# Two layers of attention and product-key experts: activation and weight stores issued from ScalarE's queue, and a reordered attention of layer 1

## The chip, the cores and the metric

The kernel runs on one core of a Trainium2 chip. A core has TensorE (PE, matrix products), VectorE (DVE), ScalarE (ACT), GpSimd (POOL) and SyncE (SP), each with an instruction stream of its own that it runs in order, and 16 DMA engines that move data between HBM and the core's memory. Transfers are issued by an engine's stream: in this kernel SP's, ACT's and, for the indexed gathers, POOL's. The metric is the device time of one launch in microseconds, the median of several.

## What is computed

Two layers, each with an attention half and an expert half. The input is a latent stream of 512 tokens and a context of 256, both 1024 wide, all in 32-bit floats.

```python
for l in range(DEPTH):                    # DEPTH = 2
    last = l == DEPTH - 1
    ...                                   # sh1 .. g2, csh1 .. cg2: (silu(c) @ w_mod[l] + b_mod[l]), six parts
    hc = modulate(h_ctx, csh1, cs1)       # rms(x) * (1 + scale) + shift
    ...                                   # keys and values of the context; last: nothing else of it
    hx = modulate(x, sh1, s1)
    q, k, v, u = split_cols(hx @ w_in[l])
    q = apply_rope(rms(q...) * q_gain[l], cos, sin)
    k = apply_rope(rms(k...) * k_gain[l], cos, sin)
    o_attn = attend_latent(q, [kc, k], [vc, v])
    o_conv = conformer_conv(u, conv_w[l], conv_b[l], ln_g[l], ln_b[l])   # 31 taps
    x = x + g1 * merge_groups(o_attn, o_conv, beta_attn[l], beta_conv[l], w_o[l])
    x = x + g2 * peer(modulate(x, sh2, s2), peer_wq[l], peer_keys[l], peer_u[l], peer_v[l])
    if not last:
        ...                               # the same for the context
return rms(x) * final_g
```

`peer` picks, for each token and each of 8 heads, 16 of 16384 experts by the sum of two key scores. For each chosen expert e it adds `gelu(h . u[e]) * w[e] * v[e]`.

## The kernel before

`attention_layer(l, ...)` and `peer_layer(l, ...)` are called in turn for the two layers. Both write their work as generators ("streams") whose `yield` carries an estimated length; `merge` (L212) always advances the stream whose clock is lowest, each multiplied by a pace (`T0`, `T1`, `FD` and so on, L43 on). That fixes the order in which instructions are written; a scheduler of the compiler may still move them, after which each engine's order is fixed.

**The expert half** computes most tokens densely: products of all 16384 `u` rows with the tokens (the u stage), then weighted sums of all `v` rows (the v stage). Every 32-bit operand is split in a high and a low part and three products are summed. In layer 0 four tiles of 128 latent tokens go this way, in layer 1 three. The rest, the two context tiles in layer 0 and the last latent tile in layer 1, is gathered: for each of the 128 expert slots of a tile, POOL gathers rows `uv` (L896), DVE forms the dot product (L900), ACT the gelu (L901, L902) and DVE adds (L889).

The u stage (`u_stream`, L978 on) takes 128 chunks of 128 experts per layer. For a chunk SP loads `raw` (L986, 512 KB, two buffers), ACT casts it to `hi` (L989), POOL makes `lo` (L990), PE runs 24 products into `ups` (L994), ACT makes `ge` (L996, two buffers), and the result is stored to `gd` in HBM (L998, 256 KB in layer 0, 192 KB in layer 1, for 120 of the 128 chunks; the last eight stay on the core). The v stage reads `gd` and `wd` back.

Beside the u stage `w_stream` spreads the router's weights over the experts. For four tokens at a time DVE makes one-hot tables `o` (L955), ACT scales one of them (L960), PE multiplies both (`wps`, L961) and ACT copies the result into `sg` (L963). After 32 tokens the block of 2 MB is stored to `wd` (L965), 16 times in layer 0 (984.6 to 1480 us) and 12 times in layer 1 (3039 to 3460 us). All `raw` loads and all `gd` and `wd` stores are issued from SP's queue.

**The attention half.** At its start `rope`, `convw` and `gains` are loaded behind the three `wqkv` blocks (L278 to L286); from gains and rope DVE makes `gq` and the four tables `rot` (L289 to L296). Then `project` (L590) runs the projections, `taps` the convolution on DVE and partly GpSimd, `largest` the row maxima. In layer 1 `context_kv` (L575) computes keys and values of one context tile: a norm (`hC`), a row broadcast through `dg` and PE (`rows`, L196 and L197), and `qkv`. It is called for the first tile inside `project` and for the second after the merge, in one piece with high priority. `more_mods` computes the modulation vectors `mods[l, s]` (L127): products of `silu(c)` with streamed blocks `wm`. At the end `conv_norm` normalizes the convolution's output into `yhi` and `ylo`, `attend` writes the attention's output into `qs` as a high part (ACT, L485) and a low part (DVE, L486), and the loop at L692 multiplies both with the split output weights (`whi` on ACT, L618; `wlo` on POOL, L619).

Of the kernel before, what the change touches and what calls it, by code (L numbers as in the profile page):

```python
# [9 lines left out]
F32 = mybir.dt.float32  # L10
# [7 lines left out]
P = 128  # L18
D = 1024
KD = D // P  # L20
# [3 lines left out]
NL = SEQ // P  # L24
NT = T // P
HD = 64
# [12 lines left out]
EPS = 1e-6  # L39
# [5 lines left out]
T0 = (1.0, 1.0)  # L45
T1 = (2.0, 2.0)
CY = 2.0
# [13 lines left out]
def body(ctx: ExitStack, tc: tile.TileContext, io):  # L61
# [165 lines left out]
    def attention_layer(l, st, fgs, fp, mark):  # L227
# [18 lines left out]
        work = pool("awk", 2, hst)  # L246
        hT = hp.tile([P, KD, nq * P], F32, tag="hT", name="hT")
        TW = SEQ if last else GW - 2 * PAD
        parts = [] if last else [(1, CT, [hT[:, k, SEQ:] for k in range(KD)])]
# [30 lines left out]
        convw = mid.tile([P, 4, CONVK], F32, name="convw")  # L280
        gains = hp.tile([P, 2, HD], F32, name="gains")

        wqkv = [wload(io["w_qkv"][l, c], "wqkv") for c in range(3)]
        nc.sync.dma_start(convw, io["convw"][:, l])
        nc.sync.dma_start(rope, io["rope"].rearrange("(n p) c d -> p n c d", p=P))
        nc.sync.dma_start(gains, io["gains"][l].partition_broadcast(P))  # L286

# [201 lines left out]
        def more_mods():  # L489
            for m in (((0, 2), (0, 3), (0, 4), (0, 5), (1, 0), (1, 1)) if l == 0 else ((1, 2), (1, 3), (1, 4), (1, 5))):  # L490
                yield from mod(*m, ppt)

        def conv_norm(t0, n, g0):
# [29 lines left out]
            for b in range(4):  # L523
                if t0:
                    V.scalar_tensor_tensor(yT[:, b, ys], yT[:, b, ys], vecs[:, l, b, 4:5], bc, op0=ALU.mult, op1=ALU.mult)
                else:
# [7 lines left out]
                    V.tensor_tensor(out=lo[:, 0:SEQ].rearrange("p (j t) -> p j t", j=hi.shape[1]), in0=q, in1=hi.bitcast(F32), op=ALU.subtract)  # L534
                    ylo.append(lo[:, 0:SEQ])
            done.append("latent" if t0 == 0 else "context")
            yield 2.0
# [39 lines left out]
        def context_kv(i):  # L577

            x = xT[:, :, i * P:(i + 1) * P]
            A.activation(hC, x, AF.Square)  # L580
            bc = rows(rsqrt(col_sums([hC[:, k, :] for k in range(KD)], 1), 1, 1.0 / D, EPS, "n"), 1)
            V.tensor_tensor(out=hC, in0=x, in1=bc.unsqueeze(1).to_broadcast([P, KD, P]), op=ALU.mult)
            V.tensor_tensor(out=hC, in0=hC, in1=mods[l, 1][:, :, 1:2].to_broadcast([P, KD, P]), op=ALU.mult)
            V.tensor_tensor(out=hC, in0=hC, in1=mods[l, 0][:, :, 1:2].to_broadcast([P, KD, P]), op=ALU.add)
            for _ in qkv(i):
                pass

        def project():
            for i in LAT if last else CT + LAT:
                yield from qkv(i)  # L590
                if last and i == LAT[-1]:
                    context_kv(NL)
            if last:
# [11 lines left out]
        if last:  # L605
            clock["mod"] = 100.0
            del streams["conv"]
            merge({**streams, "fg": (fgs, FD), "mod": (md, 2.4)}, clock, ("p", "fg"))
            with tc.high_priority():
                context_kv(NL + 1)  # L610
        else:
            merge(streams, clock, ("p",))
# [80 lines left out]
        for hf in range(4):  # L693
            if hf == len(ws):
                ws.append(wo_split(hf, op.tile([P, KD, WC], F32R, tag="whi", name="whi"), op.tile([P, KD, WC], F32R, tag="wlo", name="wlo")))
            while len(opened) < len(ws):
                opened.append(pbig.tile([P, 2, SEQ], F32, tag="big", name="wo"))
                products(opened[-1], ws[len(opened) - 1], (4, 5, 6, 7))
            ps = opened[hf]
            products(ps, ws[hf], (0, 1, 2, 3))  # L700
# [6 lines left out]
    def peer_layer(l, fp):  # L707
# [6 lines left out]
        with ExitStack() as outer:  # L714
# [216 lines left out]
            def w_stream():  # L931

                for i in dd:
# [16 lines left out]
                    for blk in range(4):  # L950
                        sg = rw.tile([P, PK // 2, 32, 2], F32, tag="sg", name="sg", bufs=2)
                        for t0 in range(0, 32, 4):
# [11 lines left out]
                            yield 1.9  # L964
                        nc.sync.dma_start(wd[:, :, (i - dd[0]) * 4 + blk].rearrange("g p h t e -> p g (h t e)"), sg.rearrange("p (g h) t e -> p g (h t e)", h=2))  # L965

# [15 lines left out]
            def u_stream():  # L982

                for c in range(PK):
# [12 lines left out]
                    if c < PK - 8:  # L997
                        nc.sync.dma_start(gd[c // 4, :, c % 4], ge[:, 0:td])  # L998
                    else:
# [189 lines left out]
```

## Time and profile before

| what | us |
|---|---|
| median of 3 runs | 4179.64 (4172.8 to 4183.14) |
| the profiled execution | 4177.53 |
| its span | 4175.8 |
| layer 0: attention, u stage, v stage | 0 to 508, to 1572, to 2316 |
| layer 1: attention, u stage, v stage | 2316 to 2725, to 3555, to 4176 |
| busy: PE, DVE, POOL, ACT | 3769, 3098, 2217, 1812 |

The profile comes from one execution on the chip, whose own time stands in the second row. A row of the timeline names the start, the length, the engine, the line of the kernel, the operation, what it writes and reads, and in brackets how long the engine stood idle before it and what released it. An engine's name with a q (SPq, ACTq) means its instruction queue, where issues of transfers are seen. A row of the waits names who waited for what, how long in all, how often, and the longest. [...]

### The profile page before, as it was taken

The page shows a single profiled execution, that of the slowest core. Times are in us where ns is not written, and L with a number is a line of the kernel's source. Part 1 is how long each engine was busy: PE and PEld are TensorE (multiplying, and loading weights), DVE is VectorE, ACT ScalarE, POOL GpSimd, SP SyncE. Part 2 cuts the span into 40 slices and gives each one's busy share as a digit, 9 for nine tenths or more (in the row PEclk, how much of TensorE's full clock was granted, in tenths as well). Part 3 has the DMA queues.
Part 4 walks back from the last instruction along what each step waited for, and adds up shares of the span by engine and source line. Part 5 has one row for each costly group of instructions (what it writes and reads, how often), then busy time and mean ns, then how long its engine had stood idle before and what let it go on. Part 6 is the DMA issues. An engine that isn't in the chain of part 4 may idle for free. (4 is left out here: it accounts for less than half of the span.)

```text
span 4175.8 us, 54192 instructions
## 1 busy us (share of the span) xinstructions
PE 3769.0 (90%) x19278; PEld 3204.7 (77%) x19278; DVE 3098.4 (74%) x5680; ACT 1811.6 (43%) x3679; POOL 2216.7 (53%) x1223
## 2 busy tenths in 40 slices
PE   8879998989988999999999779889888989898998
PEld 6547776867777777888777547679888888898897
DVE  5693369999986647898887784389877453787885
ACT  3345233336675633333333246333466564333333
POOL 0580135666665456555556356135756555665664
PEclk9989999999999999999999889899999999999999
DMA  4142135987888888988887714046676878898884
GB/s 169 58 182 81 51 119 204 331 304 244 285 285 287 268 319 338 344 322 335 339 335 292 275 41 172 21 136 241 231 247 220 259 262 283 320 345 297 315 319 140
DMA packets 327631, 1003.72 MB, mean 240 GB/s; under 512 B 24384, under 2 KB 159808, under 8 KB 264256
## 3 DMA queue, kind: packets, MB, share of 16 engines
q1 hardware_dynamic: 266128, 580.25, 40.5%
q0 software_dynamic: 59904, 419.46, 27.1%
q8 instruction: 152, 2.49, 0.2%
q14 instruction: 119, 0.97, 0.1%
q10 hardware_dynamic: 1328, 0.55, 0.0%
HBM read 884.29 MB, written 115.87 MB: 240 GB/s over the span
## 5 line engine op out<-in xcount | busy, mean ns | idle before, releaser
L990 POOL TENSOR_TENSOR lo<-raw,hi 128x1024 fp32r<-128x1024 f32 x256 | 647.1, 2529 | 572.0 <-ACT hi L989 504.7
L1028 POOL TENSOR_TENSOR vlo<-vr,vhi 128x1024 fp32r<-128x1024 f32 x256 | 629.5, 2466 | 471.4 <-ACT vhi L1027 457.4
L1035 PE MATMUL vps<-ahi,vhi 128*128 128x512 f32 (+1 forms) x2048 | 759.7, 372 | 44.5 <-DVE xT L1038 26.5
L1035 PE MATMUL vps<-alo,vhi 128*128 128x512 f32 (+1 forms) x2048 | 757.4, 370 | 3.1 <-DVE alo L974 3.1
L1035 PE MATMUL vps<-ahi,vlo 128*128 128x512 f32 (+1 forms) x2048 | 740.2, 371 | 9.2 <-POOL vlo L1028 9.1
L900 DVE SCALAR_TENSOR_TENSOR uv<-uv,hp 128x1024 f32<-128x1024 f32 x363 | 439.7, 1211 | 212.2 <-DMA uv<-in_uv,uix 212.1
L994 PE MATMUL ups<-hhi,hi 128*128 128x512 f32 (+1 forms) x2048 | 504.9, 386 | 72.2 <-ACT ge L996 34.7
L889 DVE SCALAR_TENSOR_TENSOR yp<-uv,act,yp 128x1024 f32<-128x1024 f32 x359 | 460.4, 1283 | 144.9 <-ACT act L902 144.0
L896 POOL DMA_INDIRECT uv<-in_uv,uix x384 | 447.8, 1166 | 222.0 <-DVE y L889 45.4
L994 PEld LDWEIGHTS ups<-hhi,hi 128*128 128x128 f32 x2048 | 383.7, 198 | 127.6 <-ACT ge L996 41.3
L994 PE MATMUL ups<-hhi,lo 128*128 128x512 f32 (+1 forms) x2048 | 479.0, 371 | 1.8 <-POOL lo L990 1.8
L994 PE MATMUL ups<-hlo,hi 128*128 128x512 f32 (+1 forms) x2048 | 475.1, 370 | 0.0
L1035 PEld LDWEIGHTS vps<-ahi,vhi 128*128 128x128 f32 x2048 | 391.3, 191 | 99.8 <-DVE xT L1038 30.6
L1035 PEld LDWEIGHTS vps<-ahi,vlo 128*128 128x128 f32 x2048 | 389.7, 191 | 63.2 <-POOL vlo L1028 16.2
L1035 PEld LDWEIGHTS vps<-alo,vhi 128*128 128x128 f32 x2048 | 391.6, 191 | 51.4 <-DVE alo L974 4.4
L901 ACT ACTIVATE act<-dots 128x1 f32<-128x1 f32 x384 | 77.4, 202 | 803.5 <-DVE uv L900 802.5
L994 PEld LDWEIGHTS ups<-hlo,hi 128*128 128x128 f32 x2048 | 378.8, 192 | 40.5
L994 PEld LDWEIGHTS ups<-hhi,lo 128*128 128x128 f32 x2048 | 373.4, 191 | 40.6 <-POOL lo L990 2.4
L955 DVE TENSOR_TENSOR o<-iota,xf 128x1024 f32<-128x1024 f32 x224 | 385.9, 1749 | 21.0 <-ACT o L960 9.3
L410 POOL TENSOR_TENSOR yT<-yT,tp 128x512 f32<-128x512 f32 (+1 forms) x150 | 261.4, 1743 | 211.9 <-ACT tp L409 201.7
L989 ACT CAST hi<-raw 128x1024 fp32r<-128x1024 f32 x256 | 267.0, 1043 | 217.8 <-DMA raw<-in_uT 185.3
L960 ACT ACTIVATE o<-o,wT 128x128 f32<-128x128 f32 x896 | 285.1, 392 | 152.2 <-DVE o L955 150.7
(281 smaller groups left out, 6055.0 us busy)
## 6 DMA issues: line engine op xcount, KB each, us to landing
raw<-in_uT SPq DMA_DIRECT2D x256, 512.0 KB, 4.9
vr<-in_vq SPq DMA_DIRECT2D x256, 512.0 KB, 6.0
wd<-sg SPq DMA_DIRECT2D x28, 2048.0 KB, 13.5
wm<-in_w_mod SPq DMA_DIRECT2D x48, 1024.0 KB, 6.5
w<-wd SPq DMA_DIRECT2D x32, 1024.0 KB, 6.6
gd<-ge SPq DMA_DIRECT2D x120, 256.0 KB, 6.2
ge<-gd SPq DMA_DIRECT2D x60, 512.0 KB, 7.1
w<-wd SPq DMA_DIRECT2D x32, 768.0 KB, 6.2
```

What stands on the lines that cost most here:

```text
L410: G.tensor_tensor(out=y, in0=y, in1=tp, op=ALU.add)
L889: V.scalar_tensor_tensor(y, t[:, 1, :], act[:, e:e + 1], y, op0=ALU.mult, op1=ALU.add)
L896: got = G.indirect_dma_start(out=t.rearrange("p c d -> p (c d)"), out_offset=None, in_=io["uv"], in_offset=bass.IndirectOffsetOnAxis(ap=ui ...
L900: V.scalar_tensor_tensor(t[:, 0, :], t[:, 0, :], 1.0, at["h"], op0=ALU.mult, op1=ALU.mult, accum_out=dots[:, ec])
L901: A.activation(act[:, ec], dots[:, ec], AF.Gelu)
L955: V.tensor_tensor(out=oh, in0=iota.unsqueeze(1).unsqueeze(1).to_broadcast([P, 2, 4, PK]), in1=c2[:, :, tt].to_broadcast([P, 2, 4, PK]), op ...
L960: A.activation(o2[:, j, :], o2[:, j, :], AF.Copy, scale=wT[:, t:t + 1])
L989: A.copy(hi, raw)
L990: mark.append(G.tensor_tensor(out=lo, in0=raw, in1=hi.bitcast(F32), op=ALU.subtract))
L994: PE.matmul(ps[:, 0:td], a[:, k, :], b[:, k, :], start=k == 0 and n == 0, stop=k == KD - 1 and n == 2)
L1028: mark.append(G.tensor_tensor(out=vlo, in0=raw, in1=vhi.bitcast(F32), op=ALU.subtract))
L1035: PE.matmul(ps[:, 0:td], a[:, c % 4, d * P:(d + 1) * P], b, start=c == 0 and n == 0, stop=c == 7 and n == 2)
```

## The change

It has five parts.

1. The two stores `gd` and `wd` are issued on ACT's queue in place of SP's.
2. The load of `gains` is written at the head of `attention_layer`, into a buffer of the small pool, and the load of `rope` ahead of the `wqkv` loads.
3. `mod(1, 5)` leaves the stream `more_mods` of layer 1 and is run inside the output projection's loop, in its first pass, between the convolution's products and attention's.
4. In layer 1 `context_kv` becomes a generator with pauses; the second context tile's becomes a stream `k` of the merge, which starts when the first one and the gathers written there are done, and no longer a block with high priority. `conv_norm` pauses after each `ylo`.
5. The pace of one tap stream of layer 0 goes from 2.0 to 2.6.

```diff
@@ -43,7 +43,7 @@
 FA0, FB0, FC0 = 6.2, 6.2, 6.2
 FD = 2.9
 T0 = (1.0, 1.0)
-T1 = (2.0, 2.0)
+T1 = (2.6, 2.0)
 CY = 2.0
 CP = 1.5
 NF = 5
@@ -245,6 +245,8 @@
         hp = pool("ah", 1, hst)
         work = pool("awk", 2, hst)
         hT = hp.tile([P, KD, nq * P], F32, tag="hT", name="hT")
+        gains = sm.tile([P, 2, HD], F32, tag="dg", name="gains")
+        nc.sync.dma_start(gains, io["gains"][l].partition_broadcast(P))
         TW = SEQ if last else GW - 2 * PAD
         parts = [] if last else [(1, CT, [hT[:, k, SEQ:] for k in range(KD)])]
         parts.append((0, LAT, [hT[:, k, 0:SEQ] for k in range(KD)]))
@@ -278,12 +280,10 @@
                 modulate(l, 0, v, [a[:, P:] for a in h] if last else h)
         rope = cp.tile([P, NL, 2, HD], F32, tag="tp", name="rope")
         convw = mid.tile([P, 4, CONVK], F32, name="convw")
-        gains = hp.tile([P, 2, HD], F32, name="gains")
+        nc.sync.dma_start(rope, io["rope"].rearrange("(n p) c d -> p n c d", p=P))
 
         wqkv = [wload(io["w_qkv"][l, c], "wqkv") for c in range(3)]
         nc.sync.dma_start(convw, io["convw"][:, l])
-        nc.sync.dma_start(rope, io["rope"].rearrange("(n p) c d -> p n c d", p=P))
-        nc.sync.dma_start(gains, io["gains"][l].partition_broadcast(P))
 
         gq = kp.tile([P, 2, HD], F32, tag="gq", name="gq")
         V.tensor_scalar(gq[:, 0], gains[:, 0], HD ** -0.5, None, op0=ALU.mult)
@@ -487,7 +487,7 @@
                 yield 1.0
 
         def more_mods():
-            for m in (((0, 2), (0, 3), (0, 4), (0, 5), (1, 0), (1, 1)) if l == 0 else ((1, 2), (1, 3), (1, 4), (1, 5))):
+            for m in (((0, 2), (0, 3), (0, 4), (0, 5), (1, 0), (1, 1)) if l == 0 else ((1, 2), (1, 3), (1, 4))):
                 yield from mod(*m, ppt)
 
         def conv_norm(t0, n, g0):
@@ -533,6 +533,8 @@
                     lo = cp.tile([P, gw], F32R, tag="gp", name="ylo", bufs=4)
                     V.tensor_tensor(out=lo[:, 0:SEQ].rearrange("p (j t) -> p j t", j=hi.shape[1]), in0=q, in1=hi.bitcast(F32), op=ALU.subtract)
                     ylo.append(lo[:, 0:SEQ])
+                    if last:
+                        yield 4.5
             done.append("latent" if t0 == 0 else "context")
             yield 2.0
 
@@ -578,18 +580,24 @@
 
             x = xT[:, :, i * P:(i + 1) * P]
             A.activation(hC, x, AF.Square)
-            bc = rows(rsqrt(col_sums([hC[:, k, :] for k in range(KD)], 1), 1, 1.0 / D, EPS, "n"), 1)
+            ps = small([P, P], "cs4")
+            spread(ps, [(ones[:, 0:32], hC[:, k, :]) for k in range(KD)], P)
+            yield 3.0
+            r = rsqrt(fold(ps, 1), 1, 1.0 / D, EPS, "n")
+            yield 8.0
+            bc = rows(r, 1)
             V.tensor_tensor(out=hC, in0=x, in1=bc.unsqueeze(1).to_broadcast([P, KD, P]), op=ALU.mult)
             V.tensor_tensor(out=hC, in0=hC, in1=mods[l, 1][:, :, 1:2].to_broadcast([P, KD, P]), op=ALU.mult)
             V.tensor_tensor(out=hC, in0=hC, in1=mods[l, 0][:, :, 1:2].to_broadcast([P, KD, P]), op=ALU.add)
-            for _ in qkv(i):
-                pass
+            yield 5.0
+            yield from qkv(i)
+            done.append(i)
 
         def project():
             for i in LAT if last else CT + LAT:
                 yield from qkv(i)
                 if last and i == LAT[-1]:
-                    context_kv(NL)
+                    yield from context_kv(NL)
             if last:
                 for b in range(4):
                     yield from glu([b])
@@ -605,9 +613,17 @@
         if last:
             clock["mod"] = 100.0
             del streams["conv"]
-            merge({**streams, "fg": (fgs, FD), "mod": (md, 2.4)}, clock, ("p", "fg"))
-            with tc.high_priority():
-                context_kv(NL + 1)
+
+            def gathered():
+                yield from fgs
+                done.append("fg")
+
+            def late_context():
+                while not {"fg", NL}.issubset(done):
+                    yield 1.0
+                yield from context_kv(NL + 1)
+
+            merge({**streams, "fg": (gathered(), FD), "mod": (md, 2.4), "k": (late_context(), 1.0)}, clock, ("p", "k"))
         else:
             merge(streams, clock, ("p",))
         hst.close()
@@ -696,6 +712,10 @@
             while len(opened) < len(ws):
                 opened.append(pbig.tile([P, 2, SEQ], F32, tag="big", name="wo"))
                 products(opened[-1], ws[len(opened) - 1], (4, 5, 6, 7))
+            if last and not hf:
+
+                for _ in mod(1, 5, ppt):
+                    pass
             ps = opened[hf]
             products(ps, ws[hf], (0, 1, 2, 3))
             for d in range(2):
@@ -962,7 +982,7 @@
 
                             A.copy(sg[:, :, t0:t0 + 4, :].rearrange("p i t e -> p t i e"), ps.rearrange("p t (i e) -> p t i e", e=2))
                             yield 1.9
-                        nc.sync.dma_start(wd[:, :, (i - dd[0]) * 4 + blk].rearrange("g p h t e -> p g (h t e)"), sg.rearrange("p (g h) t e -> p g (h t e)", h=2))
+                        nc.scalar.dma_start(wd[:, :, (i - dd[0]) * 4 + blk].rearrange("g p h t e -> p g (h t e)"), sg.rearrange("p (g h) t e -> p g (h t e)", h=2))
 
             def weighted(vp, act, w):
 
@@ -995,7 +1015,7 @@
                     ge = up.tile([P, 512], F32, tag="ge", name="ge")
                     A.activation(ge[:, 0:td], ps[:, 0:td], AF.Gelu)
                     if c < PK - 8:
-                        nc.sync.dma_start(gd[c // 4, :, c % 4], ge[:, 0:td])
+                        nc.scalar.dma_start(gd[c // 4, :, c % 4], ge[:, 0:td])
                     else:
                         if c % 4 == 0:
                             w = weights(vpa[0], c // 4)
```

In the changed kernel the lines stand 2 to 20 further on: the `wd` store at L985, the `gd` store at L1018, `raw` at L1006, `hi` at L1009, `ge` at L1016, `o` at L980, `sg` at L983, the gathered tile's gelu at L921 and L922, `whi` at L634, and the normalization of `hT` at L270.

SP's order around one `wd` store in layer 0, before the change:

```order
L986 DMA raw<-in_uT 128x1024 x2
L998 DMA gd_3289<-ge 128x512 x2
L986 DMA raw<-in_uT 128x1024
L965 DMA wd_3290<-sg 128x32x128
L998 DMA gd_3289<-ge 128x512
L986 DMA raw<-in_uT 128x1024
L998 DMA gd_3289<-ge 128x512
```

In the changed kernel neither store is left in SP's order, whose rows go from 792 to 304. ACT's order around the first `wd` store there:

```order
L1016 ACTIVATE ge<-ups 128x512
L921 ACTIVATE act<-dots 128x1
L985 DMA wd_3290<-sg 128x32x128
L1018 DMA gd_3289<-ge 128x512
L922 ACTIVATE act<-act,wk 128x1
L980 ACTIVATE o_6230<-o_6230,wT 128x128 x4
L983 COPY sg<-wps 128x4x64x2
L1009 CAST hi<-raw 128x1024
L980 ACTIVATE o_6276<-o_6276,wT 128x128 x4
L1016 ACTIVATE ge<-ups 128x512
```

Both stores now stand between ACT's own instructions; between a `wd` and the next `gd` there are none here, in other places up to some twenty.

DVE's order at the start of layer 1's attention, before (`dg` is the row broadcast's diagonal, `rbc` its result, `hT` the normalized input of `qkv`):

```order
L196 TENSOR_TENSOR dg<-ident,rs_y 128x512
L289 TENSOR_SCALAR gq<-gains 128x64
L290 COPY gq<-gains 128x64
L268 TENSOR_TENSOR hT<-xT,rbc 128x8x128
L204 TENSOR_TENSOR hT<-xT,rbc 128x384 x8
L293 TENSOR_TENSOR rot<-rope,gq 128x4x64
```

and after:

```order
L196 TENSOR_TENSOR dg<-ident,rs_y 128x512
L293 TENSOR_TENSOR rot<-rope,gq 128x4x64
L296 TENSOR_TENSOR rot<-rope,gq 128x4x32 x2
L293 TENSOR_TENSOR rot<-rope,gq 128x4x64
L296 TENSOR_TENSOR rot<-rope,gq 128x4x32 x2
L270 TENSOR_TENSOR hT<-xT,rbc 128x8x128
L204 TENSOR_TENSOR hT<-xT,rbc 128x384 x8
```

`gq` has moved up to before the norm's sums, and the six `rot` operations from behind `hT` to ahead of it. In SP's order the three `wqkv` loads, `convw` and `rope` still follow each other in this sequence, and `gains` is gone from behind them.

ACT's order ahead of layer 1's output projection, before (`osq` and `o` are the norm of attention's output, `sq` the squares of the next norm, `m` the copy of a modulation's products):

```order
L469 ACTIVATE osq,oss<-o 128x512 x4
L475 ACTIVATE o<-o,rs_y 128x512 x4
L485 CAST qs<-of 128x4x128 x2
L618 CAST whi<-wo 128x2048 x2
L485 CAST qs<-of 128x4x128 x2
L174 ACTIVATE sq<-xT 128x512 x8
```

and after:

```order
L469 ACTIVATE osq,oss<-o 128x512 x4
L475 ACTIVATE o<-o,rs_y 128x512 x4
L485 CAST qs<-of 128x4x128 x4
L135 COPY m_19834<-mp_19813 128x512
L634 CAST whi<-wo 128x2048
L135 COPY m_19863<-mp_19842 128x512
L174 ACTIVATE sq<-xT 128x512 x2
L634 CAST whi<-wo 128x2048
```

All four `qs` casts now come first; the two `whi` casts follow, each behind a copy of `mod(1, 5)`.

## Rows read from the trace of the kernel before

**Rows 1.** Windows: length; PE, PEld, DVE, ACT, POOL busy; PEclk; DMA share, GB/s.

```profile
980.00:1300.00 320.00, 290.11 (x1542) 245.10 (x1542) 297.50 (x338) 216.91 (x565) 200.09 (x94) 0.98 0.86 276
1300.00:1500.00 200.00, 178.24 (x905) 149.98 (x904) 114.43 (x117) 113.88 (x291) 94.16 (x48) 0.95 0.86 287
3035.00:3480.00 445.00, 389.54 (x2340) 381.76 (x2340) 269.96 (x239) 261.34 (x644) 249.68 (x116) 0.95 0.77 251
```

**Rows 2.** Timeline of SP's queue at two weight stores.

```profile
1385.20 0.37 SPq L965 DMA_DIRECT2D wd<-sg  x1
1385.67 9.02 SPq L986 DMA_DIRECT2D raw<-in_uT  x1
...
3115.22 0.37 SPq L965 DMA_DIRECT2D wd<-sg  x1
3115.68 11.44 SPq L998 DMA_DIRECT2D gd<-ge  x1
```

**Rows 3.** One line at a time: the weight stores and the table loads.

```profile
L965 SPq DMA_DIRECT2D wd<-sg x28: 370/371/686, 984.6 to 3460.3; - x28
...
L986 SPq DMA_DIRECT2D raw<-in_uT x256: 327/333/11621, 508.5 to 3539.0; - x128
```

**Rows 4.** Waits of ACT in the three windows: us, times, longest.

```profile
ACT hi L989 <- DMA raw<-in_uT: 11.6, 4, 10.0
...
ACT hi L989 <- DMA raw<-in_uT: 51.7, 8, 13.5
...
ACT hi L989 <- DMA raw<-in_uT: 61.5, 21, 9.1
```

**Rows 5.** Waits of PE, 1300 to 1500 and then 3035 to 3480.

```profile
PE ups L994 <- ACT ge L996: 13.5, 2, 6.9
...
PE wps L961 <- ACT sg L963: 31.0, 14, 5.6
PE ups L994 <- ACT hi L989: 14.1, 3, 6.0
```

**Rows 6.** Timeline of PE after one such wait.

```profile
3293.48 2.93 PE L994 MATMUL ups<-hhi,hi 128*128 128x384 f32 x8 [5.95 <-ACT hi L989]
3297.71 1.55 PE L994 MATMUL ups<-hhi,lo 128*128 128x384 f32 x8
```

**Rows 7.** Groups of ACT's instructions by line, 3035 to 3480.

```profile
L960 ACT ACTIVATE o<-o,wT 128x128 f32<-128x128 f32 x348 | 110.3, 393 | 57.4 <-DVE o L955 56.8
L989 ACT CAST hi<-raw 128x1024 fp32r<-128x1024 f32 x68 | 70.8, 1041 | 66.5 <-DMA raw<-in_uT 61.5 <-PE ups L994 4.7
```

**Rows 8.** Timeline of the first microsecond: one issue on each queue.

```profile
0.75 0.41 ACTq L94 DMA_DIRECT2D vecs<-in_vecs  x1
0.75 0.40 SPq L87 DMA_DIRECT2D cT<-in_cT  x1
```

**Rows 9.** Timeline of SP, DVE and PE at the start of layer 1.

```profile
2318.53 0.44 SPq L285 DMA_DIRECT2D rope<-in_rope  x1
2319.39 0.33 SPq L286 DMA_DIRECT2D gains<-in_gains  x1
...
2338.70 0.20 DVE L289 TENSOR_SCALAR gq<-gains 128x64 f32<-128x64 f32 x1 [13.30 <-DMA gains<-in_gains]
...
2347.75 1.65 PE L319 MATMUL qkv<-wqkv,hT 128*128 128x256 f32 x3 [18.73 <-DVE rs_y L148]
```

**Rows 10.** Waits of PE 2440 to 2500, and one window of it.

```profile
PE rows L197 <- DVE dg L196: 8.6, 1, 8.6
...
2460.00:2480.00 20.00, 10.02 (x28) 7.13 (x29) 19.72 (x28) 6.23 (x13) 7.49 (x5) 0.50 0.00 1
```

**Rows 11.** Timeline of DVE ahead of the output projection; the waits of PE there.

```profile
2677.33 1.29 DVE L486 TENSOR_TENSOR qs<-of,qs 128x512 fp32r<-128x512 f32 x2 [0.33 <-ACT qs L485]
2682.11 7.69 DVE L486 TENSOR_TENSOR qs<-of,qs 128x512 fp32r<-128x512 f32 x2 [2.28 <-ACT qs L485]
...
PE wo L689 <- DVE qs L486: 6.0, 1, 6.0
```

## The prediction

> **What bounds the kernel now.** I read the windows of the profile first, to see which engine sets the pace where the stores move. TensorE is busy for 90% of the run, but less in the three stretches in which the one-hot expert weights are made beside the u products: 290 of 320 us, 178 of 200 and 390 of 445 [rows 1]. In the first VectorE is nearly as full (297.5 us), so there VectorE sets the pace; in the other two no engine is full and 21.8 + 55.5 = 77 us of TensorE lie idle. Next I read SyncE's queue around one weight store. The store of `wd` takes 0.37 us to issue, and the instruction behind it then takes 9.02 or 11.44 us where it normally takes 0.33 [rows 2, 3]. This is so behind all 28 of these stores: a `raw` load comes next 12 times, a `gd` store 16 times, and together they hold SyncE for 161 us. Counted from the issue of `wd`, the queue goes on after about 8.2 us on average (6 to 12.5). Behind no `gd` store alone is there such a hold. A held queue means a late `raw`: the waits of ScalarE show 11.6 + 51.7 + 61.5 = 125 us for it in the three windows [rows 4]. ScalarE runs its instructions in order, so what it does for others stands behind the late cast, and the waits of TensorE name it: `ups` on `ge`, `wps` on `sg`, `ups` on `hi` [rows 5].
>
> **What the held queue costs today.** Going through the 28 stores one by one, TensorE's gaps behind them add up to 27 us in layer 0 and 37 us in layer 1. After such a gap it is slow for a while: the first eight products took 2.93 us and eight of the next group 1.55 [rows 6], 1.4 us more. With some 16 such gaps that is about 22 us. So the whole price, and the most that the move of the stores can return, is 27 + 37 + 22 = 86 us, or 0.69 us for each of the 125 us that ScalarE is held.
>
> **Moving the stores.** SyncE keeps only loads in these stages, so no `raw` stands behind a `wd` in its queue: if the two queues are independent, the 125 us go. But a hold of the queue that carries the store does not vanish. In ScalarE's new order `wd` is followed by the next `gd`, and that is now what is held, with all of ScalarE's work behind it. Between the two stand 0 to 9.1 us of ScalarE's work, 3.1 us on average over the 28 (a few scalings at 0.39 us, a cast at 1.04 us and the like [rows 7]). ScalarE is busy 592 of 965 us in these windows, 61% [rows 1], so 3.1 us of work last about 5.1 us. With the release at 8.2 us the hold is 3.1 us where all are alike; taken one by one, with none below zero, about 3.6 us, 100 us in all. With a release at 9.5 us it would be 125. At the old rate of 0.69 that costs 69 us. I take less, 52, because the hold now begins while `raw` keeps coming and TensorE still has the split of the next chunk ready, 24 products of 3 x 1.55 = 4.65 us [rows 6], of which I let 3 us count as cover for each hold. If the release comes before the `gd` issue the cost is nothing; if the cover is gone, as in rows 6, it is 69 to 86.
>
> The 240 `gd` issues cost ScalarE itself time as well. An issue takes 0.41 us on ScalarE's queue [rows 8], so 98 us in the run. Some 60 us of that lie in the three windows, where ScalarE has 39% to spare; outside them it is busy for less than half of the time. I put 12 us of it on the path, between 0 and 30. The term for the stores is thus -86 + 52 + 12 = -22 us, with ends of -86 and +35, the last from the rival below. SyncE has nothing else that waits for these stores, and GpSimd's gathers are not moved past them.
>
> **The pace of the taps (2.0 to 2.6 in layer 0).** In the order of VectorE the 60 taps stand at the same places among the reductions as before, so it costs nothing; the cover is that order itself. A pace that did bite would show in layer 0's attention, and I allow 3 us either way.
>
> **Gains and rope.** At the start of layer 1 VectorE stands 13.3 us at `gq` for the gains, and TensorE 18.7 us at `qkv` behind it [rows 9]. The change brings the gains early. But in the new order the six `rot` operations, which read rope, stand ahead of the normalization that `qkv` needs, and rope keeps its place behind the three `wqkv` loads and `convw` in SyncE's queue, one place ahead of the gains of today (2318.53 and 2319.39). So the wait changes its name and ends about as late; the rope operations, about 2 us, now come ahead of the normalization. I take 0, between -13 (rope is early after all) and +2.
>
> **The last context block.** [...] As a stream with pauses it is spread among the taps: VectorE has the same work, so only TensorE's idle time can go. Of 22 us idle between 2440 and 2500 I take half, -10, between -20 and +5 (the end if the keys of that tile are late for the scores).
>
> **Ahead of the output projection.** The second half of the `qs` differences takes 7.69 us instead of 1.29, beside GpSimd's split of `wo`, and TensorE waits 6.0 us for it [rows 11]. In the new order ScalarE does all four `qs` casts before the first `whi` cast, so the split starts later and does not fall beside them. Moved in is `mod(1, 5)`: four products of about 1 us, whose loads have come long before. That is -8, between -12 and +2.
>
> **The sum.** Attention: 0 - 10 - 8 = -18. With the stores: -22 - 18 = -40. The profiled run of before took 4177.5 us, so 4137.5; the median of the runs shown is 2 us above that, which gives 4140.
>
> **Rivals.** A is this forecast: the queues are independent and the hold moves to ScalarE at a lower price; 4115 to 4168.
>
> B: the hold is not the queue's but that of something both queues share. Then `raw` is held as it is today, and ScalarE is held at `gd` on top of that. Nothing of the 86 us returns. The hold on ScalarE is partly the same time as the wait for `raw` that follows, so I charge 23 us for the products and weights that ScalarE can't feed meanwhile, plus the 12 us of issues: +35 - 18 = +17, or 4197. It turns slower as soon as this extra is above 18 us. It speaks for it that all rows behind `wd` are from the one queue, so none shows a free second queue; against it stands only that two issues at 0.75 us overlapped on the two queues, at 0.41 and 0.40 us [rows 8], but both were small transfers.
>
> [...] It has a chance of about 3 in 10 here, since rows 8 don't show such a wait but could not show it for a store of 2 MB.
>
> C: the queues are independent but ScalarE's hold has no cover. 125 us at 0.69 are 86, as much as `raw` costs now, and the issues come on top: -86 + 86 + 12 - 18 = -6, or 4174. In favour: in-order ScalarE feeds every consumer here.
>
> D: the hold ends before `gd` nearly always, because a queue without `raw` behind it drains sooner: -86 + 12 - 18 = -92, or 4088.
>
> **How the numbers follow.** A 0.42, B 0.32, C 0.13, D 0.13. A difference below about 0.3%, 12.5 us, can't be told from no change; so faster is below 4167 and slower above 4192. Faster: A 0.36, C 0.04, D 0.13, together 0.53. Same: A 0.05, C 0.07, B 0.13, together 0.25. Slower: A 0.01, C 0.02, B 0.19, together 0.22. The likeliest case gives 4140. The range reaches from just below D, 4085, to a little above B, 4202; beyond it lie about half of D and a fifth of B.
>
> **What would show it.** The `raw` issues of SyncE behind each `wd`: 0.33 us says A, C or D; 6 to 12 us says B. The `gd` issues on ScalarE behind `wd`: holds of 100 us in all say A, of 125 and TensorE gaps like those of rows 5 say C, of below 20 say D. ScalarE's waits for `raw` in the three windows: from 125 us to below 30, except in B. At layer 1's start a DVE wait of some 13 us for rope in place of the one for the gains. Between 2440 and 2500 fewer idle microseconds of TensorE, and 1.3 us for the late `qs`. The forecast is wrong if the two holds add up, if ScalarE's holds cost TensorE more than half of their time, or if attention does not give about 18 us.

## The result, and the profile after

The changed kernel takes 4210.7 us, the median of four runs (4187 to 4221), against 4181.4 us for the kernel before in the same rounds: 1.0063 times as long, with an interval of 1.0037 to 1.0089. The forecast was 4140, in a range of 4085 to 4202. The profiled execution is the fastest of the four, 4187.3 us with a span of 4185.3, so its trace shows only 9.5 of the 29 us that the median lost; the experiments have to tell the rest.

Cut at the first and last products of each stage (not the borders of the table of the time before), the traces give these lengths in us:

| stage | before | after |
|---|---|---|
| layer 0, attention (to the first `ups` product) | 525.9 | 542.8 |
| layer 0, u stage | 1045.9 | 1057.0 |
| of it, first to last `wps` product | 522.8 | 534.3 |
| layer 0, v stage | 744.6 | 742.8 |
| layer 1, attention | 422.7 | 412.3 |
| layer 1, u stage | 815.0 | 807.2 |
| of it, first to last `wps` product | 449.0 | 429.5 |
| layer 1, v stage and end | 621.7 | 623.2 |

Three readings stand out, and only one of them was forecast: 17 us more in layer 0's attention, 10 less in layer 1's, and almost nothing gained in the two u stages together (+3).

**The stores.** The lines of both, in the changed kernel's numbering (least, median and longest issue in ns):

```profile
L1018 ACTq DMA_DIRECT2D gd<-ge x240: 325/326/10942, 558.5 to 3525.8; - x120
...
L1006 SPq DMA_DIRECT2D raw<-in_uT x256: 327/328/647, 525.2 to 3550.5; - x128
```

No `raw` load takes more than 0.65 us to issue, where it was up to 11.6 [rows 3]. The hold now falls on `gd` in ScalarE's queue, up to 10.9 us. ScalarE's timeline at one store in layer 0, and last the row of SyncE that falls into the hold:

```profile
1435.60 0.38 ACTq L985 DMA_DIRECT2D wd<-sg  x1
...
1440.28 10.94 ACTq L1018 DMA_DIRECT2D gd<-ge  x1
1451.27 1.08 ACT L983 COPY sg<-wps 128x512 f32<-128x512 f32 x2 [11.01 <-issue]
...
1442.07 0.33 SPq L1006 DMA_DIRECT2D raw<-in_uT  x1
```

Here the next `gd` takes 10.94 us, and the copy of `sg` behind it starts after 11.01 us in which ScalarE did nothing; "issue" as the releaser means that the profile shows nothing that it waited for, and the `gd` ahead of it on ScalarE's own queue ends at 1451.22, 0.05 us before the copy starts. In the middle of this hold SyncE issues a `raw` in 0.33 us. The same happens behind most of the 28 stores: 24 of the `gd` issues behind them take over 2 us, 140 us in all, and the 14 `raw` loads issued inside these holds take 0.33 us each. ScalarE's waits for `raw` have shrunk to 17 us from 125 [rows 4], in the three windows of the same work:

```profile
ACT hi L1009 <- DMA raw<-in_uT: 4.4, 2, 3.3
...
ACT hi L1009 <- DMA raw<-in_uT: 2.1, 1, 2.1
...
ACT hi L1009 <- DMA raw<-in_uT: 10.5, 6, 3.0
```

In the second of them TensorE's longest wait has changed its name and kept its size (13.9 us for `sg`, 13.5 for `ge` before); in the third the same two waits are shorter, 29 us in place of 45 [rows 5]:

```profile
PE wps L981 <- ACT sg L983: 13.9, 4, 6.5
...
PE wps L981 <- ACT sg L983: 21.0, 15, 6.0
PE ups L1014 <- ACT hi L1009: 7.9, 2, 4.2
```

And the windows themselves (the columns as in [rows 1]; PEclk is the granted clock of TensorE as a share of its full speed) show TensorE busy for 88, 93 and 91% of the time, against 91, 89 and 88%, and idle for 96 us in all, against 107:

```profile
980.00:1320.00 340.00, 299.79 (x1549) 253.77 (x1548) 286.47 (x351) 215.28 (x558) 200.89 (x98) 0.95 0.80 264
1320.00:1525.00 205.00, 190.09 (x990) 161.91 (x989) 136.09 (x125) 125.01 (x323) 105.13 (x52) 0.97 0.88 290
3045.00:3485.00 440.00, 398.89 (x2412) 387.79 (x2410) 273.06 (x246) 270.41 (x664) 255.60 (x118) 0.96 0.78 260
```

**Layer 1's attention.** The wait at its start has changed its name from gains to rope and kept its length, and `qkv` waits 18.38 us where it was 18.73 [rows 9]; the late `qs` takes 1.29 us in place of 7.69 [rows 11]. DVE, PE and DVE again:

```profile
2365.18 0.42 DVE L293 TENSOR_TENSOR rot<-rope,gq 128x256 f32<-128x256 f32 x1 [12.98 <-DMA rope<-in_rope]
...
2374.20 2.08 PE L319 MATMUL qkv<-wqkv,hT 128*128 128x256 f32 x4 [18.38 <-DVE rs_y L149]
...
2700.00 1.29 DVE L486 TENSOR_TENSOR qs<-of,qs 128x512 fp32r<-128x512 f32 x2
```

**Layer 0's attention.** The window from 460 to 480 us, of the kernel before and then of the changed one:

```profile
460.00:480.00 20.00, 20.00 (x91) 16.38 (x90) 4.22 (x7) 6.22 (x6) 9.21 (x2) 1.00 0.13 27
```

```profile
460.00:480.00 20.00, 6.74 (x24) 4.47 (x23) 15.13 (x20) 5.02 (x5) 8.99 (x2) 0.68 0.12 26
```

TensorE stands idle for 13 of these 20 us. The timeline there (DVE, POOL, PE):

```profile
464.01 4.35 DVE L154 SCALAR_TENSOR_TENSOR rs_t<-rs_t,rs_v 128x4 f32<-128x4 f32 x1
468.40 4.42 DVE L155 SCALAR_TENSOR_TENSOR rs_y<-rs_t,rs_y 128x4 f32<-128x4 f32 x1
...
473.05 0.16 DVE L154 SCALAR_TENSOR_TENSOR rs_t<-rs_t,rs_v 128x4 f32<-128x4 f32 x1
...
463.81 8.99 POOL L635 TENSOR_TENSOR wlo<-wo,whi 128x2048 fp32r<-128x2048 f32 x2 [60.65 <-DVE rs_y L155]
...
474.35 2.05 PE L197 MATMUL rows<-dg,ones 128*128 128x512 f32 x2 [11.77 <-DVE dg L196]
```

The latent stream's last normalization now runs when everything else of the attention is done, just beside GpSimd's split `wlo`. Two operations on 128 x 4 elements take 4.35 and 4.42 us there, where the next from the same line takes 0.16; the second ends at 472.82, as the split does at 472.80. TensorE waits 11.77 us for the broadcast that follows. The latent `yf`, ready at 433 us before, is ready at 480.

### The profile page after: what moved, and what is told of

The parts are those of the page before. It is cut to its first block, busy times and chain, and to the rows that moved or that the text cites. A ratio compares the mean times of both kernels' runs of the same rounds, so it can differ in the third digit from the quotient of the medians.

```text
span 4185.3 us, 54070 instructions
## 1 busy us (share of the span) xinstructions
PE 3772.1 (90%) x19278; PEld 3203.8 (77%) x19278; DVE 3060.3 (73%) x5680; ACT 1804.4 (43%) x3672; POOL 2219.0 (53%) x1223
## 5 line engine op out<-in xcount | busy, mean ns | idle before, releaser
L921 ACT ACTIVATE act<-dots 128x1 f32<-128x1 f32 x384 | 77.3, 201 | 765.3 <-DVE uv L920 747.4
L975 DVE TENSOR_TENSOR o<-iota,xf 128x1024 f32<-128x1024 f32 x224 | 377.5, 1709 | 32.4 <-PE wps L981 14.6
L980 ACT ACTIVATE o<-o,wT 128x128 f32<-128x128 f32 x896 | 283.7, 392 | 142.9 <-DVE o L975 123.5
L1009 ACT CAST hi<-raw 128x1024 fp32r<-128x1024 f32 x256 | 266.8, 1043 | 158.2 <-DMA raw<-in_uT 100.1
```

The lines of the kernel that those rows point to most:

```text
L975: V.tensor_tensor(out=oh, in0=iota.unsqueeze(1).unsqueeze(1).to_broadcast([P, 2, 4, PK]), in1=c2[:, :, tt].to_broadcast([P, 2, 4, PK]), op ...
L980: A.activation(o2[:, j, :], o2[:, j, :], AF.Copy, scale=wT[:, t:t + 1])
L1009: A.copy(hi, raw)
```

## The experiments

Times are medians with the ratio to the kernel before in the same rounds. A kernel's runs spread by 10 to 40 us, so a difference of two medians is good to about 5 us.

| kernel | median us | ratio | interval |
|---|---|---|---|
| e1: the change, both stores on SyncE again | 4191.2 | 1.0017 | 0.9998 to 1.0037 |
| e2: before, both stores on ScalarE | 4206.2 | 1.0062 | 1.0040 to 1.0084 |
| e3: before, `wd` on ScalarE | 4148.1 | 0.9916 | 0.9883 to 0.9948 |
| e12: the same again | 4153.7 | 0.9929 | 0.9911 to 0.9947 |
| e5: before, `gd` on ScalarE | 4197.4 | 1.0040 | 1.0026 to 1.0055 |
| e4: the change, pace 2.0 | 4206.3 | 1.0057 | 1.0033 to 1.0082 |
| e6: before, pace 2.6 | 4205.8 | 1.0063 | 1.0039 to 1.0087 |
| e10: the change, stores and pace as before | 4187.8 | 1.0008 | 0.9991 to 1.0024 |
| e13: before, gains and rope moved | 4194.8 | 1.0036 | 1.0019 to 1.0052 |
| e14: before, context stream and pauses | 4177.1 | 0.9994 | 0.9977 to 1.0012 |
| e7: the change, pace 2.0, `gd` on SyncE | 4155.0 | 0.9941 | 0.9924 to 0.9959 |
| e16: the same again | 4150.1 | 0.9923 | 0.9900 to 0.9945 |
| e11: as e7, gains and rope not moved | 4132.0 | 0.9873 | 0.9859 to 0.9888 |
| e15: the same again | 4133.7 | 0.9892 | 0.9864 to 0.9919 |

e8 (4134.1) and e9 (4167.8) have one run each.

### The four ways to place two stores: e2, e3, e5

```diff
-                        nc.sync.dma_start(wd[:, :, (i - dd[0]) * 4 + blk]...   # e2, e3 and e12
+                        nc.scalar.dma_start(wd[:, :, (i - dd[0]) * 4 + blk]...
-                        nc.sync.dma_start(gd[c // 4, :, c % 4], ge[:, 0:td])   # e2 and e5
+                        nc.scalar.dma_start(gd[c // 4, :, c % 4], ge[:, 0:td])
```

> The kernel before with nothing changed but the two stores, which are issued from ScalarE. Theory (a hold moved from SyncE to ScalarE at nearly the same price): the u stages take 1046 + 0 to 13 and 815 - 9 to 0 us, the time is 4170 to 4190. ScalarE is held at gd behind wd for 100 to 150 us in all, no raw issue takes over 1 us. Rival (the move returns what the late raw cost, and the changed kernel lost it elsewhere): below 4150.

> The kernel before with only the 2 MB store wd issued from ScalarE; gd stays on SyncE. Theory (the hold falls on whatever transfer stands next in the queue that carries wd, and the queues are independent): the next transfer in ScalarE's queue is the next wd, 20 us later or more, so nobody is held; raw and gd issue in 0.33 us. The gaps of TensorE behind wd go, 4095 to 4130. Rival (TensorE's gaps there come from the transfer's own load on the DMA engines, or from VectorE's pace): raw lands late all the same and the time stays at 4160 to 4180.

> The kernel before with only the 240 gd stores issued from ScalarE; the 28 wd stores stay on SyncE. SyncE's next transfer behind a wd is now always a raw load, which is held as before, and ScalarE issues 240 times at about 0.33 us, 79 us of its time. Theory (ScalarE's own issue time is nearly all hidden, the price in the change is the hold): 4178 to 4192, and the stretch from the first to the last expert-weight product stays near the 523 and 449 us of before, within 8 us each. Rival (the issues on ScalarE are the price): 4195 to 4215, with that stretch 10 us or more longer in each layer.

> The kernel before with wd alone issued from ScalarE, once more and in the same rounds as the two others, to compare them with. Theory: 4141 to 4152 again, and stretches of expert-weight products near 512 and 423 us.

The windows from the first to the last `wps` product, layer 0 and layer 1, of the kernel before:

```profile
951.00:1474.00 523.00, 475.25 (x2503) 401.89 (x2502) 432.42 (x495) 341.92 (x889) 301.24 (x145) 0.97 0.84 274
3007.00:3456.00 449.00, 395.87 (x2399) 387.90 (x2400) 292.29 (x276) 276.50 (x689) 255.61 (x118) 0.95 0.75 244
```

with `wd` alone on ScalarE (e3):

```profile
953.00:1465.00 512.00, 475.98 (x2502) 402.07 (x2502) 432.15 (x499) 343.88 (x896) 298.99 (x145) 0.98 0.87 282
3002.00:3424.00 422.00, 390.45 (x2403) 382.66 (x2402) 286.44 (x276) 275.52 (x687) 256.76 (x118) 0.97 0.78 258
```

with `gd` alone (e5):

```profile
951.00:1476.00 525.00, 477.71 (x2500) 401.91 (x2499) 427.84 (x497) 343.58 (x893) 300.59 (x145) 0.96 0.84 274
3009.00:3462.00 453.00, 396.46 (x2403) 386.00 (x2404) 290.90 (x276) 277.51 (x688) 254.44 (x118) 0.95 0.75 242
```

and with both (e2):

```profile
958.00:1509.00 551.00, 483.88 (x2504) 409.76 (x2504) 424.20 (x498) 345.16 (x893) 297.85 (x145) 0.94 0.80 262
3043.00:3482.00 439.00, 394.83 (x2400) 384.02 (x2401) 289.34 (x276) 276.71 (x688) 254.59 (x118) 0.96 0.76 249
```

Together they last 972, 934, 978 and 990 us. So moving `wd` returns 38, moving `gd` costs 6, and both together cost 18, which is 50 more than the sum of the two. That 50 is put down to the hold of `gd` behind `wd`. In the whole times the same four stand at 0, -35 (-31 in e12), +17 and +24, 42 more than the sum. One trace a kernel is not sharper than that: over all kernels with the same placement these windows last 961 to 981 us (both stores on SyncE, seven traces), 928 to 938 (`wd` on ScalarE, six) and 964 to 990 (both on ScalarE, three, the changed kernel lowest), and with the means of these groups the surplus is 38. So it lies at some 40 to 50 us. The medians of e2 and e3 came out 16 and 18 us above the upper ends of what was expected. Who is held is seen in the issues. In e3, first `gd`, then `raw`:

```profile
L998 SPq DMA_DIRECT2D gd<-ge x240: 319/326/1148, 542.0 to 3492.6; - x120
...
L986 SPq DMA_DIRECT2D raw<-in_uT x256: 327/332/1355, 507.5 to 3513.8; - x128
```

and in e5, again `gd`, then `raw`:

```profile
L998 ACTq DMA_DIRECT2D gd<-ge x240: 326/326/551, 541.8 to 3526.5; - x120
...
L986 SPq DMA_DIRECT2D raw<-in_uT x256: 327/328/9612, 508.6 to 3547.2; - x128
```

Where nothing but the next `wd` follows in ScalarE's queue, no issue takes over 1.4 us. Where `wd` is SyncE's, the `raw` behind it takes up to 9.6 us while `gd` on ScalarE's queue never takes more than 0.55. The hold belongs to the queue that carries the store. e5's whole time is 10 us above what its windows show; where these are was not found, so in the whole time the 240 issues on ScalarE can cost more than 6 us.

### What of the gaps the store itself makes: e8

This kernel is e3 with a quarter of each store; it leaves out three quarters of the weights.

```diff
-wd[:, :, (i - dd[0]) * 4 + blk]
+wd[0:8, :, (i - dd[0]) * 4 + blk]        # read back as wd[g % 8]
```

> As the kernel with wd alone on ScalarE, but each wd store writes only the first 8 of 32 groups, 0.5 MB of 2 MB; the weights are read back from these 8 groups, so three quarters of the expert weights are left out of the result. The expert-weight stretches take 512 and 423 us with the whole store on ScalarE, with some 35 us of TensorE's gaps left within 20 us behind the stores. Theory (these gaps are the load of the 2 MB on the DMA engines, by which raw and the gathers land later): the stretches shrink by another 10 to 25 us together. Rival (the gaps belong to the weave of VectorE and ScalarE and only happen to lie there): within 5 us of 512 and 423.

```profile
959.00:1464.00 505.00, 472.50 (x2504) 397.40 (x2503) 422.39 (x499) 346.20 (x897) 298.95 (x146) 0.99 0.74 241
2997.00:3410.00 413.00, 387.61 (x2403) 378.23 (x2403) 285.98 (x278) 275.54 (x688) 252.51 (x117) 0.98 0.67 223
```

918 us against the 934 of e3, and against 928 to 938 of all six kernels with `wd` on ScalarE: another 10 to 20 us go with the other 1.5 MB of each store, and the DMA engines are busy for 74 and 67% of the two windows instead of 87 and 78. e3, where no issue is held any more, still pays them, so the choice of a queue does not return them.

### The pace: e6, e4 and e1

```diff
-T1 = (2.0, 2.0)
+T1 = (2.6, 2.0)      # e6; e4 is the change with this line as before
```

> The kernel before with only the tap pace of layer 0 at 2.6. Theory: the output projection of layer 0 starts at 477 to 480 us instead of 462, TensorE idles some 13 us between 460 and 480 us, the time is 4193 to 4203, 12 to 18 us above before. Rival (the later start in the changed kernel came from gains, rope or another clock of TensorE): 4180 to 4187 with the projection at about 462 us.

> The changed kernel with the tap pace of layer 0 at 2.0 again. Theory (the pace puts the last normalization of the convolution behind attention in the order, and the output projection waits for it): the first product of layer 0's u stage comes at 524 to 528 us instead of 542.8, the latent yf at about 430 instead of 476, the time is 14 to 17 us below the changed kernel's. Rival (gains and rope, or the stores, made layer 0's attention longer): no change there, 542 us.

> The changed kernel with both stores issued from SyncE again; everything else of the change stays. Theory: the profile's +9.5 us is made of +16 in layer 0's attention (the pace of the taps), -10 in layer 1's attention and +3 in the two u stages (the stores). Then this kernel's profile is at 4183 to 4187, its u stages take about 1046 and 815 us as before, and its first product of the u stage still comes at about 542 us instead of 526. Rival: the stores cost much more than the one profile shows (the runs of the changed kernel lie between 4187 and 4221); then the median here falls to about 4185 and the runs lie close together.

In e6 alone the output projection starts at 476.6 us instead of 462.4, and TensorE's waits there are those of the changed kernel, 11.8 us for the broadcast. In e4 the gap is gone:

```profile
460.00:480.00 20.00, 20.00 (x100) 17.08 (x100) 7.24 (x13) 8.74 (x10) 4.78 (x2) 1.00 0.09 37
```

Yet e4's projection starts at 472.8, not at 462 (what holds it there is told with e13), and its median lies only 4 us below the changed kernel's, which is no difference that these runs can tell. By itself the pace costs 25 us; of these the trace of e6 shows 15 in layer 0's attention. e1 shows the stores' part of the loss from the other side: 20 us, where e2 has 24.

### Layer 1's attention part by part: e10, e9, e14, e13

```diff
-            for m in (... else ((1, 2), (1, 3), (1, 4), (1, 5))):     # e9
+            for m in (... else ((1, 2), (1, 3), (1, 4))):
...
+            if last and not hf:
+                for _ in mod(1, 5, ppt):
+                    pass
```

> The changed kernel with both stores back on SyncE and the pace back at 2.0: gains, rope, context_kv, conv_norm and mod(1, 5) remain. Theory (layer 1's attention gives 10 us and nothing takes it back): 4168 to 4174. Rival (the earlier gains or the new weave cost as much elsewhere, as the kernel with wd alone on ScalarE and this attention, 4155, against 4148 without it, hints): 4178 to 4188, with layer 0's attention 3 to 10 us longer.

> The kernel before with only mod(1, 5) moved into the output projection's loop. In the changed kernel's profile layer 1's attention is 10.4 us shorter, 6.2 of it up to the end of the attention products and 4.4 in the stretch from there to the last output product. Theory (the second part is this move, by which the qs casts come ahead of the whi casts): that last stretch goes from 56.9 to about 52.5 us and the attention products end where they did, layer 1's attention 418 us. Rival (it is the reordered conv_norm and context): 422 us.

> The kernel before with only context_kv as a stream and the pauses in conv_norm. mod(1, 5) alone gave layer 1's attention its whole 10 us in a profile (412.0 instead of 422.7). Theory (the context stream gives nothing by itself: TensorE's idle time moves behind VectorE's taps): layer 1's attention 419 to 426 us, time 4178 to 4188. Rival (it gives the 10 us that I forecast for it): 410 to 414 us, 4170 to 4176.

> The kernel before with only the loads of gains and rope moved as in the change. The kernel with wd alone on ScalarE and the new attention took 4132 without the moved gains and 4155 with them. Theory (the moved loads cost some 20 us): 4195 to 4208; layer 0's attention 528 to 533 us. Rival (the two kernels lay apart by other causes): 4180 to 4187, layer 0's attention at 525 us but for a dip of TensorE's clock.

The theory fell in e10: with only the attention's edits the time is that of the kernel before. e9 and e14 separate them. `mod(1, 5)` alone brings layer 1's attention to 412.0 us, the whole gain: 4.7 us up to the last attention product, into which one product stream fewer is woven, and 6.0 behind it: the late `qs` takes 1.29 us there and TensorE no longer waits for it, while in e14 it still takes 7.69 and TensorE waits 6.0. Layer 1's attention takes 411 to 416 us in all nine traces with this move, and 419 to 427 in the nine without it. The context stream leaves it at 422.5 and the time unchanged. The 8.6 us wait for `dg` [rows 10] is gone, and TensorE waits elsewhere instead; in e14 from 2440 to 2540, and the window of [rows 10] there:

```profile
PE s L557 <- DVE gp L389: 11.1, 1, 11.1
PE kTp L364 <- ACT kk L355: 9.1, 1, 9.1
...
2460.00:2480.00 20.00, 2.48 (x6) 1.28 (x6) 19.72 (x32) 6.27 (x11) 10.41 (x8) 0.56 0.00 1
```

`gp` comes from VectorE behind a row of taps, and `kk` from ScalarE behind VectorE's `qk`. VectorE is as full in that window as before, and TensorE idles 24.8 us between 2440 and 2500, against 21.2. e13 finds what ate the gain: moving gains and rope costs 14 us. With that the parts of e10 add up: 14 - 4 - 11 = -1, and +3 was measured. In e13's trace the first `x` reaches VectorE at 9.1 us instead of 6.8, behind the gains' transfer, layer 0's attention takes 539.5 us and layer 1's 426.9. Five traces have this move with the old pace (e4, e7, e10, e13, e16; 529 to 540 us), and all five show a gap of about 3 us in TensorE between 400 and 420 us that the kernels without it lack; there the attention products and the convolution's sums are woven in another order. In two of them, e4 and e13, the granted clock falls: it is 0.84 and 0.82 (e4) and 0.91 and 0.75 (e13) from 400 to 420 and from 420 to 440 us, where e10 and e16 have 1.00 in both. With the levels 0.50 and 1.00, the only two in the traces of before and of the changed kernel, that is 13.6 us at 0.50 in each. Their output projections start 6 to 10 us later than those of the other three. So 4 to 14 us are seen in layer 0 and 0 to 4 in layer 1 (e16 against e15, e13 against before); how the 14 of the median divide over these can't be told from one trace a kernel, and by what path the late `x` leads to the other order was not found.

### A version that beats both: e7, e16, e11, e15

These are the change with the pace at 2.0 and `gd` on SyncE; e11 and e15 also load gains and rope where they were before.

> The changed kernel with the pace of 2.0 and gd on SyncE, so that only wd is issued from ScalarE and layer 1's attention is the changed one. Theory (the parts add up): 35 us below before from wd, 10 us from layer 1's attention, so 4132 to 4145. Rival (the attention's gain is given back later, as the whole time of the kernels with it suggests): 4148 as with wd alone.

> The kernel before with wd issued from ScalarE, context_kv, conv_norm and mod(1, 5) as in the change; gains and rope are loaded where they were. Theory (moving gains lengthens layer 0's attention a little and gives layer 1 nothing): layer 0's attention is at 525 us again, layer 1's at 412, the time 4133 to 4140 and below the 4155 of the kernel that has the moved gains as well. Rival (gains and rope have no part): about 4150 to 4155.

> wd alone from ScalarE, context stream and mod(1, 5) as in the change, gains and rope where they were; the same kernel once more, for the comparison with the next in the same rounds. 4128 to 4142.

> The same with gains and rope moved. Theory (they cost 20 us): 4150 to 4160. Rival (the runs of different rounds misled): within 6 us of the kernel without the move.

In the same rounds e15 is 16 us below e16, a second measure of what the moved loads cost. e11 and e15, 4132 and 4134 us, are 48 to 53 us below the kernel before: 31 to 35 from `wd`, 10 from layer 1's attention by the traces, and 3 to 12 that no trace settles. e7 came out 10 us above its expectation, which is the moved loads.

## Why the prediction was wrong

**The stores: right mechanism, one term mis-sized.** The queues are independent here: no `raw` takes more than 0.65 us to issue, and the 14 that fall into the holds of ScalarE's queue take 0.33. The hold, up to 10.94 us, moves to ScalarE, and rival B is out; its 3 in 10 was an estimate of mine, which no row of before could test. So is D, with 140 us of holds. The sum was -86 + 52 + 12 = -22. The windows above measure -38, +50 (38 by the groups of traces) and +6. The price of the hold came near, but by two errors that cancel: the holds are longer than the 100 us forecast (144 us behind the 28 stores here, 172 in e2, since `gd` comes after 3.9 us instead of 5.1 and the queue goes on after 9 to 10 us instead of 8.2), and each of their microseconds costs TensorE 0.2 to 0.35 instead of 0.52. The issues were cheaper in the windows (0.326 us each instead of 0.41), and the return was less than half of what I booked. The step that failed is "So the whole price, and the most that the move of the stores can return, is 27 + 37 + 22 = 86 us". It put down to the held queue every gap of TensorE behind a store. (One of the 28 issues behind the stores, at 0.41 us, was not even held.) With no hold at all (e3) TensorE's idle time in the windows falls from 101 to 68 us (972 - 871.1 and 934 - 866.4), so 33 return and not 64. The rest is there for other reasons, the 2 MB on the DMA engines (e8) among them. The 22 us for the slow products after a gap were worse: TensorE's busy time falls by 4.7 us. With 38 in the place of 86 the term is +26 by my own working, and 24 was measured for e2. Rival C had holds that cost as much as they return, which is near what was measured, but it got there by a higher price and not by a lower return, and it ended 37 us too low.

**The pace: wrong, by its own cover.** "In the order of VectorE the 60 taps stand at the same places among the reductions as before, so it costs nothing" was true of the taps and looked no further. The stream behind them, the convolution's last normalization, had moved behind attention in the same order. It would have been seen by following in the order what the taps feed, up to the output projection. I allowed 3 us; it is 25 alone.

**Gains and rope.** The forecast for layer 1 came true: a wait for rope of 12.98 us in place of 13.30. What I did not cost is the other end of the move, in layer 0: a load moved to the head of the queue stands ahead of `x`. It was 0 in the sum and is 14.

**The context stream.** -10 forecast, nothing found. I wrote that VectorE has the same work and then let half of TensorE's idle time go all the same. VectorE was full (19.7 of 20 us [rows 10]) and is so in e14, and TensorE's idle time went to the next operations that wait for VectorE.

**`mod(1, 5)`.** -8 forecast; -10.7 in e9's trace, 6.0 of it by the reason given, and 4.7 ahead of it, probably from the lighter weave, which I had not counted.

The parts measured alone, 24 + 25 + 14 - 4 - 11 = 48, are more than the 29 of the whole. Pace and moved loads share a part: with the pace alone the projection of layer 0 starts at 476.6 us, with the moved loads as well at 477.9, since the normalization comes last in either. That is 1.3 us later, where the moved loads alone put it 3 us later (13 in e13, with its slow clock). So 2 to 12 of the 19 us are shared; the others are not explained, and medians that are good to 5 us each leave room for them.

## What to carry to other kernels

Here a store of 2 MB held the transfer behind it in its own queue for more than 2 us, up to 11.6, in 27 of 28 cases before and in 24 of 28 in the changed kernel, and behind the stores of 192 and 256 KB no issue took more than 1.8 us in either trace. Such a store belongs in a queue where nothing urgent follows, and its small companions do not belong behind it on an engine that has other work. Before booking a stall as gain, ask what each idle gap would wait for next: here half of it had a second reason. A change of a pace or a load's place has to be followed in the new order to the last consumer, and in every layer in which it holds.

## What the runs showed of the hardware

The hold is the queue's own: up to 11.6 us on SyncE's (before) and 11.1 on ScalarE's (e2) behind a store of 2 MB, and none on the other queue at the same time: in the changed kernel 14 `raw` loads were issued inside such holds, in 0.33 us each, and in e5 no `gd` on ScalarE's queue took over 0.55 us where `raw` on SyncE's took up to 9.6.

In the changed kernel two operations of VectorE on 128 x 4 elements took 4.35 and 4.42 us beside GpSimd's two of 128 x 2048, about 27 times the 0.16 that the same lines took just before and after; the second ended at 472.82 us, GpSimd's at 472.80.

TensorE's granted clock dipped in some executions where it was busy all the time. In e2 and e8, and not in the kernel before or e3, it was 0.66 to 0.68 of full speed in one 20 us window of layer 0's attention, the order there being that of before. With the two levels 0.50 and 1.00 that is 13 to 14 us at 0.50; in e2 TensorE had been busy for all of the 20 us ahead, with a granted clock of 1.00. First e2, then e3:

```profile
380.00:400.00 20.00, 20.00 (x92) 15.22 (x90) 4.82 (x8) 6.00 (x8) 1.22 (x2) 0.66 0.03 12
```

```profile
380.00:400.00 20.00, 20.00 (x141) 16.63 (x141) 7.03 (x22) 10.11 (x12) 0.61 (x1) 1.00 0.00 1
```

In e2 the next stage starts 7 us later than in the kernel before (its first `raw` is issued at 515.2 us instead of 508.5). Dips of this kind may be a part of the spread between runs of one kernel: in the 23 runs of the kernel before beside e13 to e16 the mean granted clock lies between 0.948 and 0.956, the time between 4162 and 4192 us, and the two go together with a correlation of -0.46. By the 7 us of e2 I take a stage length from one trace to be good to several microseconds only.
